# Order of the weight sums, the first evacuation and the activation sums in a Winograd feed-forward layer

## The chip, the cores and the metric

One Trainium2 chip, one NeuronCore. The time is device microseconds of one execution; the median of the runs is the figure that is compared.

## What is computed

One layer of a hybrid encoder on 2,048 prompt rows and 32 sample rows, all in float32. Attention and a gated linear attention come first; the change lies in the feed-forward part that follows, a gated MLP with a causal convolution of width 3 between its two matrix products (D_MODEL is 1024, D_FF 2816):

```python
def conv_ffn(h, conv_state, w_up, w_dw, b_dw, w_down):
    t = h.shape[1]
    u = h @ w_up
    uu = jnp.concatenate([conv_state.astype(u.dtype), u], axis=1)
    y = b_dw
    for j in range(CONV_W):
        y = y + w_dw[j] * uu[:, j:j + t]
    a, g = jnp.split(y, 2, axis=-1)
    out = (jax.nn.gelu(a, approximate=True) * g) @ w_down
    return out, uu[:, -(CONV_W - 1):]
```

## The kernel before

**Units and blocks.** The feed-forward part runs from about 1838 us of the profiled span to its end. It is twelve units. Units 0 to 2 are the up product for the row groups p = 0, 1, 2, with 22 column pairs each; the other nine are the down product, for three row groups times three pieces g of the inner dimension, with 4 column pairs each (units 3 to 5 belong to p = 0). `block` handles one column pair. Below, up0, up1 and up2 are the three up units, and down0 the three down units of p = 0.

**One block.** Each column pair is a 2x2 block product in the Winograd form of Strassen's scheme: seven products instead of eight, of the weight operands A11, S2, S1, S3, A12, S4, A22 with the row operands B11, T2, T1, T3, B21, B22, T4. `prod` (the matmul line is L1561) is one of them: 12 matmuls on TensorE (PE), since every float32 operand is split in a high and a low part. The block's text order is: A11·B11 into ad0; ScalarE (ACT) copies ad0 to g0 (L1656); then `prev()`, the rest of the block before (its product A22·T4, its convolution of g, its gate product); then S2·T2 into g0 and the copy U2 (L1662); S1·T1 and the copy P5 (L1665); S3·T3 and the add to g1 (L1668, VectorE, DVE); A12·B21; S4·B22 and the add to ad1 (L1679, DVE). Then ad is evacuated: in an up unit by `conv` (L1575 on ACT, twice L1577 on DVE) and Gelu (L1687), in a down unit by `down_sum`.

**Side work.** Between the products stands `side()`, seven times in a block. It issues deferred transfers, steps the rows' preparation (`hstep`: loads of `ht` and their splits) and takes one step of the generator `weights()` (`next(wq)`). Such a step makes one weight operand ready: `part` calls `split`, which writes the high part on ACT (L67) and the low part on DVE (L70) into a ring of places (`hA`, `hB`, `ring`).

**Weight sums.** S1 = A21 + A22, S2 = S1 − A11, S3 = A11 − A21 and S4 = A12 − S2 are made once, in the blocks of row group 0 (22 columns of up0 and 12 of down0, 34 in all): S1, S2 and S3 by GpSimd (POOL, L1512), S4 by DVE (also L1512). They are stored to DRAM (`sW`, `sD`; L1515) and loaded again for the other row groups. The raw weights stand in eight buffers (`raws`, loads at L1490); `free` and `freed` list those to be filled.

**Activation sums.** After every second block of an up unit, `act_sums` makes the row operands' sums for the down product out of two stored activations (`work` tiles; L1599 to L1602 on DVE); the activations go to `actD`, their sums to `aT` (L1590). The sums overwrite the tile of which `actD` is written, so they wait for those stores.

**What sets the order.** A building framework schedules each engine's instructions: the text's order is the priority, and it moves an instruction up or down where its model says that another is ready first. Each engine then runs its list in that order, waiting at each entry for semaphores. Where an instruction ends up is seen in the built program alone.

Of the kernel before, what the change touches and what calls it, by code (L numbers as in the profile page):

```python
# [13 lines left out]
AF = mybir.ActivationFunctionType  # L14
# [25 lines left out]
def dap(ap, offset, dims):  # L40
    return bass.AP(tensor=ap.tensor, offset=ap.offset + offset, ap=dims)
# [17 lines left out]
def encoder_step(ctx: ExitStack, tc: tile.TileContext, I, O):  # L59
# [520 lines left out]
    with ExitStack() as st:  # L580
# [188 lines left out]
        def step(gen):  # L769
            if gen is not None:  # L770
                next(gen, None)
# [690 lines left out]
    def raw(i, n=4):  # L1462
        return raws_[:, 512 * i:512 * i + 128 * n].rearrange("p (k n) -> p k n", n=128)
# [12 lines left out]
    def weights():  # L1476


        todo = []
        for u, (p, g) in enumerate(UNITS):  # L1480
            for m in range(NM[u]):
                todo += [(u, m, x) for x in (("A21", "A22", "A11", "A12") if p == 0 else WOPS)]
        at = {}

        def fetch():

            while todo and free and len(at) < NRAW - 2:
                u, m, x = todo.pop(0)
                at[u, m, x] = i = free.pop(0)
                nc.sync.dma_start(raw(i, NK[u]), w_rows(u, m, x))  # L1490

        freed = []

        def refill():

            free.extend(freed)
            freed.clear()
            fetch()

        def part(u, m, x, i):  # L1500
# [9 lines left out]
        def total(u, m, eng, op, out, a, b):  # L1510
            n = NK[u]
            getattr(eng, op)(raw(out, n), raw(a, n), raw(b, n))  # L1512

        def keep(u, m, x, i):
            nc.sync.dma_start(w_rows(u, m, x), raw(i, NK[u]))  # L1515

        fetch()
        for u, (p, g) in enumerate(UNITS):
            for m in range(NM[u]):
                if p == 0:  # L1520
                    a11, a12, a21, a22 = [at.pop((u, m, x)) for x in ("A11", "A12", "A21", "A22")]
                    free.extend(freed)
                    freed.clear()
                    s1, s2 = free.pop(0), free.pop(0)
                    total(u, m, nc.gpsimd, "tensor_add", s1, a21, a22)
                    total(u, m, nc.gpsimd, "tensor_sub", s2, s1, a11)
                    total(u, m, nc.gpsimd, "tensor_sub", a21, a11, a21)
                    fetch()
                    for x, i in zip(WOPS, (a11, s2, s1, a21, a12, a12, a22)):
                        if x == "S4":  # L1530
                            total(u, m, nc.vector, "tensor_sub", a12, a12, s2)
                            freed.append(s2)
                        yield from part(u, m, x, i)
                        if x == "S1":
                            keep(u, m, "S2", s2)
                        if x in SUM and x != "S2":
                            keep(u, m, x, i)
                        yield
                        refill()
                        if x not in ("S2", "A12"):  # L1540
                            freed.append(i)
                else:
                    for x in WOPS:
                        i = at.pop((u, m, x))
                        yield from part(u, m, x, i)
                        yield
                        refill()
                        freed.append(i)

    wq = weights()  # L1550

# [40 lines left out]

    def act_sums():

        while made:
            p, j, x, y = made.pop(0)
            o = WP[p] - 2
            x0, x1, y0, y1 = x[:, 0, :o], x[:, 1, :o], y[:, 0, :o], y[:, 1, :o]
            nc.vector.tensor_sub(x0, x1, x0)  # L1599
            nc.vector.tensor_sub(x1, y1, x1)  # L1600
            nc.vector.tensor_sub(y1, y1, x0)
            nc.vector.tensor_sub(y0, y0, y1)  # L1602
            for i, v in ((0, x), (2, y)):
                defer(0 if p == 2 and j == MF // 2 - 1 else 1,
                      dap(aT, ((4 * p + i) * 11 + j) * 128 * SEG, [[SEG, 128], [11 * 128 * SEG, 2], [1, o]]), v[:, :, :o])

    def up_g(p, m, g, ya, before):

        o = WP[p] - 2
        conv(YG, g, m + MF, o)  # L1610
        nc.vector.tensor_mul(ya[:, :, :o], ya[:, :, :o], YG[:, :, :o])
        defer(1, actD[p, m, :, :, :o], ya[:, :, :o])
        if m % 2:
            made.append((p, m // 2, before, ya))

    xs = {}
    ORDER = (0, 4, 1, 5, 2, 6, 3, 7)
# [26 lines left out]
    def block(u, m, prev, side):  # L1644
# [27 lines left out]
        if u == 2:  # L1672
            conv_outputs(g[:, 1], m + MF)
# [6 lines left out]
        if u == 2:  # L1680
            conv_outputs(ad[:, 1], m)
        if grp is None:
            YA.append(YA.pop(0))
            before, ya = YA[-2:]
            o = w - 2
            conv(ya, ad, m, o)
            nc.scalar.activation(ya[:, :, :o], ya[:, :, :o], AF.Gelu_apprx_tanh)  # L1687
        else:
# [131 lines left out]
    def side():  # L1820
        issue()
        step()
        next(wq, None)
        hstep()
        pend()

    f2 = prev = None
    for u, (p, grp) in enumerate(UNITS):
        for m in range(NM[u]):
# [15 lines left out]
            if u == 0 and f2 is None and not queue:  # L1845
                s3.close()
                f2 = pool(ctx, "ff2")
                fr = f2.tile([128, 2 * 1024], F32R, name="ring")
                sa, sq = [f2.tile([128, 2, SEG], F32, name=x) for x in ("saF", "sqF")]
                acc2 = f2.tile([128, 12 * SEG], F32, name="acc2")  # L1850
                spare = [x[:, 2 * SEG * c:2 * SEG * c + 2 * SEG].rearrange("p (s w) -> p s w", w=SEG)
                         for x, n in ((work, 5), (acc2, 6)) for c in range(n)]
# [72 lines left out]
```

## Time and profile before

| | before |
|---|---|
| median of 3 runs | 3352.89 us (3344.52 to 3361.07) |
| profiled execution, own time | 3328.72 us |
| its span | 3327.0 us |
| mean granted clock of TensorE | 0.981 |
| busy: PE, DVE, ACT, POOL | 94%, 68%, 50%, 17% |

The span is the time that the trace covers, the own time that of the same execution as the runs are timed; it is 24 us below the runs' median. The granted clock is a share of TensorE's full speed.

### The profile page before, as it was taken

To read this page: it belongs to the slowest core of one execution; us is meant where nothing else is said; L and a number is where in the kernel's file an instruction comes from. 1 tells how busy PE (TensorE), PEld (TensorE's weight loads), DVE (VectorE), ACT (ScalarE), POOL (GpSimd) and SP (SyncE) were. 2 spreads that over 40 slices of the span, in tenths; PEclk is the share of its full clock that TensorE was granted. 3 is DMA by queue.
4 is the path that set the end of the run, shared out by engine and by line. 5 is a ranking of instruction groups with operands and counts; after the bars stand their busy time and mean duration, and the time that the engine had idled before them with its cause. 6 is when DMAs were issued, how large, how long until landed. Compare 5 with 4: busy or idle time off the path is not lost. (4 is left out here: it accounts for less than half of the span.)

```text
span 3327.0 us, 58007 instructions
## 1 busy us (share of the span) xinstructions
PE 3134.7 (94%) x19928; PEld 2979.6 (90%) x19928; DVE 2264.7 (68%) x4858; ACT 1673.4 (50%) x3835; POOL 573.0 (17%) x687
## 2 busy tenths in 40 slices
PE   6999999999999999899999798999999999899996
PEld 5899998888999999889988787999999999899996
DVE  6725527664545555754777887887778778788886
ACT  4412224443455545533545644465556656566755
POOL 3102101111111111112444323210000001221011
PEclk8999999999999999999999999999999999999998
DMA  7334434445333333654565786576668666769794
GB/s 216 113 121 142 128 110 120 126 129 138 107 109 113 111 106 114 206 169 155 166 213 172 234 263 223 189 238 193 185 183 242 192 191 194 232 208 294 222 284 125
DMA packets 601370, 580.25 MB, mean 174 GB/s; under 512 B 55761, under 2 KB 529570, under 8 KB 601074
## 3 DMA queue, kind: packets, MB, share of 16 engines
q1 hardware_dynamic: 556386, 528.93, 53.1%
q10 hardware_dynamic: 44432, 47.34, 4.4%
q8 instruction: 157, 2.57, 0.3%
q14 instruction: 139, 1.14, 0.1%
q0 software_dynamic: 256, 0.26, 0.0%
HBM read 388.71 MB, written 187.65 MB: 173 GB/s over the span
## 5 line engine op out<-in xcount | busy, mean ns | idle before, releaser
L76 PE MATMUL pm<-hA,wh 128*128 128x416 f32 x768 | 288.2, 375 | 0.0
L67 ACT ACTIVATE hA<-raws 128x512 fp32r<-128x512 f32 (+1 forms) x320 | 196.5, 617 | 180.7 <-PE ad L1561 96.8
L77 PE MATMUL pm<-hA,wh 128*128 128x416 f32 x768 | 269.4, 351 | 0.0
L78 PE MATMUL pm<-hA,wl 128*128 128x416 f32 x768 | 269.2, 351 | 0.0
L1561 PE MATMUL ad<-hA,hB 128*128 128x350 f32 (+2 forms) x1533 | 264.4, 323 | 0.9 <-ACT work L1665 0.7
L1561 PEld LDWEIGHTS ad<-hA,hB 128*128 128x128 f32 x1533 | 249.4, 189 | 1.8 <-ACT work L1665 1.7
L1512 POOL TENSOR_TENSOR raws<-raws 128x512 f32<-128x512 f32 (+1 forms) x102 | 147.6, 1460 | 587.2 <-DVE g L1571 284.6
L70 DVE TENSOR_TENSOR hA<-raws,hA 128x512 fp32r<-128x512 f32 (+1 forms) x320 | 229.6, 720 | 28.0 <-ACT hA L67 26.8
L67 ACT ACTIVATE hB<-raws 128x512 fp32r<-128x512 f32 (+1 forms) x240 | 147.0, 616 | 131.2 <-PE ad L1561 68.0
L934 POOL TENSOR_SCALAR P<-P,mx 128x640 f32<-128x640 f32 (+5 forms) x136 | 101.3, 745 | 544.0 <-DVE mx L933 269.1
L1561 PE MATMUL g<-hA,hB 128*128 128x350 f32 (+2 forms) x954 | 171.8, 330 | 20.4 <-ACT g L1656 9.7
L1561 PE MATMUL ad<-hA 128*128 128x350 f32 (+2 forms) x1047 | 182.9, 325 | 2.0 <-ACT work L1665 2.0
L70 DVE TENSOR_TENSOR hB<-raws,hB 128x512 fp32r<-128x512 f32 (+1 forms) x240 | 168.6, 705 | 22.9 <-ACT hB L67 20.8
L1561 PEld LDWEIGHTS g<-hA,hB 128*128 128x128 f32 x954 | 157.6, 192 | 26.5 <-ACT g L1656 13.4
L76 PE MATMUL pn<-wh,hA 128*128 128x256 f32 (+1 forms) x624 | 177.8, 285 | 0.0
L1561 PE MATMUL ad<-hA,hA 128*128 128x348 f32 (+2 forms) x1014 | 177.8, 325 | 0.0
L78 PE MATMUL pn<-wh,hA 128*128 128x256 f32 (+1 forms) x624 | 176.7, 283 | 0.0
L77 PE MATMUL pn<-wl,hA 128*128 128x256 f32 (+1 forms) x624 | 176.7, 283 | 0.0
L1561 PEld LDWEIGHTS ad<-hA 128*128 128x128 f32 x1047 | 171.8, 191 | 2.3 <-ACT work L1665 2.3
L1561 PE MATMUL ad<-hA,ring 128*128 128x348 f32 (+2 forms) x978 | 169.5, 324 | 1.3 <-ACT work L1665 1.3
L67 ACT ACTIVATE pth<-pp 128x256 fp32r<-128x256 f32 (+1 forms) x288 | 106.1, 373 | 126.3 <-PE pp L1001 116.3
L1561 PEld LDWEIGHTS ad<-hA,hA 128*128 128x128 f32 x1014 | 166.6, 191 | 0.1
(437 smaller groups left out, 9168.9 us busy)
## 6 DMA issues: line engine op xcount, KB each, us to landing
raws<-in_w_up_dram SPq DMA_DIRECT2D x220, 256.0 KB, 3.7
raws<-sW SPq DMA_DIRECT2D x176, 256.0 KB, 3.0
sW<-raws SPq DMA_DIRECT2D x88, 256.0 KB, 3.2
raws<-in_w_down_dram SPq DMA_DIRECT2D x80, 256.0 KB, 4.6
wr<-in_w_in_dram SPq DMA_DIRECT2D x76, 256.0 KB, 3.4
sgT<-tx ACTq DMA_DIRECT2D x80, 208.0 KB, 2.3
wa<-in_w_ada_dram SPq DMA_DIRECT2D x64, 256.0 KB, 3.1
keys<-ks SPq DMA_DIRECT2D x128, 128.0 KB, 2.9
```

Source lines behind the costliest of these rows:

```text
L67: i = nc.scalar.activation(hi, src, AF.Copy)
L70: nc.vector.tensor_sub(lo, src, f32(hi))
L76: nc.tensor.matmul(out, ah, bh, start=first and i == 0, stop=False)
L77: nc.tensor.matmul(out, ah, bl, start=False, stop=False)
L78: nc.tensor.matmul(out, al, bh, start=False, stop=last and i == n - 1)
L934: nc.gpsimd.tensor_scalar(P[:m, :tot], P[:m, :tot], mx[:m, 6:7], 1.0, op0=OP.mult, op1=OP.mult)
L1512: getattr(eng, op)(raw(out, n), raw(a, n), raw(b, n))
L1561: nc.tensor.matmul(out[:, :w], l_[:, k], r_[:, k, :w], start=first and k == 0 and i == 0, stop=k == n - 1 and i == 2, skip_group_check=True)
```

## The change

It edits five things. (1) `weights()` is written anew: GpSimd's three sums of a column are emitted at operand S4 of the column before (`total3(cur + 1)`), only column 0's still right before its own use; S4 is computed at operand S3 and written over S2's buffer instead of A12's; each sum's store stands right behind its split; loads are emitted for no more than one column ahead, without the earlier limit of six buffers. (2) The evacuation of ad (`conv`, Gelu, `conv_outputs`, or `down_sum`) moves into `rest()`, so that in the text it stands after the next block's first product and copy. (3) `act_sums` runs one column pair later, and its stores are always deferred by one step. (4) `side()` calls `hstep()` ahead of `next(wq)`. (5) The list of spare row buffers of one stage begins with the other tensor.

```diff
-        todo = []
-        for u, (p, g) in enumerate(UNITS):
-            for m in range(NM[u]):
-                todo += [(u, m, x) for x in (("A21", "A22", "A11", "A12") if p == 0 else WOPS)]
-        at = {}
+        cols = [(u, m) for u in range(len(UNITS)) for m in range(NM[u])]
+        fresh = [UNITS[u][0] == 0 for u, m in cols]
+        todo = [(c, x) for c in range(len(cols)) for x in (("A21", "A22", "A11", "A12") if fresh[c] else WOPS)]
+        at, freed = {}, []
+        cur = -1
         def fetch():
-            while todo and free and len(at) < NRAW - 2:
-                u, m, x = todo.pop(0)
-                at[u, m, x] = i = free.pop(0)
-                nc.sync.dma_start(raw(i, NK[u]), w_rows(u, m, x))
+            while todo and free and todo[0][0] <= cur + 1:
+                c, x = todo.pop(0)
+                at[c, x] = i = free.pop(0)
+                nc.sync.dma_start(raw(i, NK[cols[c][0]]), w_rows(*cols[c], x))
...
+        def total3(c):
+            free.extend(freed)
+            freed.clear()
+            at[c, "S1"], at[c, "S2"] = s1, s2 = free.pop(0), free.pop(0)
+            at[c, "S3"] = a21 = at.pop((c, "A21"))
+            total(c, nc.gpsimd, "tensor_add", s1, a21, at[c, "A22"])
+            total(c, nc.gpsimd, "tensor_sub", s2, s1, at[c, "A11"])
+            total(c, nc.gpsimd, "tensor_sub", a21, at[c, "A11"], a21)
...
-                    s1, s2 = free.pop(0), free.pop(0)
-                    total(u, m, nc.gpsimd, "tensor_add", s1, a21, a22)
-                    total(u, m, nc.gpsimd, "tensor_sub", s2, s1, a11)
-                    total(u, m, nc.gpsimd, "tensor_sub", a21, a11, a21)
-                    fetch()
-                    for x, i in zip(WOPS, (a11, s2, s1, a21, a12, a12, a22)):
-                        if x == "S4":
-                            total(u, m, nc.vector, "tensor_sub", a12, a12, s2)
-                            freed.append(s2)
-                        yield from part(u, m, x, i)
-                        if x == "S1":
-                            keep(u, m, "S2", s2)
-                        if x in SUM and x != "S2":
-                            keep(u, m, x, i)
-                        yield
-                        refill()
...
+        for cur in range(len(cols)):
+            u, m = cols[cur]
+            for x in WOPS:
+                if x == "A11" and fresh[cur] and (cur, "S1") not in at:
+                    total3(cur)
+                if x == "S3" and fresh[cur]:
+                    at[cur, "S4"] = at[cur, "S2"]
+                    total(cur, nc.vector, "tensor_sub", at[cur, "S4"], at[cur, "A12"], at[cur, "S4"])
+                if x == "S4" and cur + 1 < len(cols) and fresh[cur + 1]:
+                    total3(cur + 1)
+                i = at[cur, x]
+                yield from part(cur, x, i)
+                if fresh[cur] and x in SUM:
+                    nc.sync.dma_start(w_rows(u, m, x), raw(i, NK[u]))
+                yield
+                refill()
...
     def act_sums():
-        while made:
+        if made and made[0] is None:
+            made.pop(0)
+        elif made:
             p, j, x, y = made.pop(0)
...
         if m % 2:
-            made.append((p, m // 2, before, ya))
+            made.extend((None, (p, m // 2, before, ya)))
...
         nc.vector.tensor_add(ad[:, 1, :w], ad[:, 1, :w], U2[:, :w])
-        if grp is None:
-            YA.append(YA.pop(0))
-            before, ya = YA[-2:]
-            o = w - 2
-            conv(ya, ad, m, o)
-            nc.scalar.activation(ya[:, :, :o], ya[:, :, :o], AF.Gelu_apprx_tanh)
-        else:
+        if last:
             down_sum(p, grp, m, ad, m == 0)
         side()
 
         def rest():
+            if grp is None:
+                YA.append(YA.pop(0))
+                before, ya = YA[-2:]
+                o = w - 2
+                if u == 2:
+                    conv_outputs(ad[:, 1], m)
+                conv(ya, ad, m, o)
+                nc.scalar.activation(ya[:, :, :o], ya[:, :, :o], AF.Gelu_apprx_tanh)
+            elif not last:
+                down_sum(p, grp, m, ad, m == 0)
             prod(g[:, 0], u, m, "A22", "T4", False)
...
     def side():
         issue()
         step()
+        hstep()
         next(wq, None)
-        hstep()
         pend()
```

The built programs show where this puts the instructions. First ACT, in up0, from the evacuation of one block's ad to the copy U2 of the next (that is block 15 of 22), before:

```order
L1575 ACTIVATE work_22385<-ad_24428,cw_21930 128x2x348 [waits DMAHW7_49,DVE_49]
L67 ACTIVATE hB1_677<-raws_21938 128x512 [waits PE_49,Pool_49]
L1656 COPY g_24571<-ad_24570 128x350 [waits PE_49,Activation_49]
L67 ACTIVATE hB1_677<-raws_21938 128x512 [waits PE_49,Pool_49]
L1687 ACTIVATE work_22385<-work_22385 128x2x348 [waits DVE_49]
L1575 ACTIVATE work_22385<-g_24429,cw_21930 128x2x348 [waits PE_49]
L67 ACTIVATE hA0_104<-raws_21938 128x512 [waits PE_49,Pool_49]
L1662 COPY work_22385<-g_24571 128x350 [waits PE_49,Activation_49]
```

The same place of the changed program (its lines for L1575, L1687 are L1571, L1690):

```order
L1571 ACTIVATE work_22386<-ad_24425,cw_21930 128x2x348 [waits DMAHW0_49,DVE_49]
L67 ACTIVATE hB1_677<-raws_21938 128x512 [waits PE_49,Pool_49]
L1656 COPY g_24562<-ad_24561 128x350 [waits PE_49,Activation_49]
L67 ACTIVATE hB1_677<-raws_21938 128x512 [waits PE_49,Pool_49]
L1690 ACTIVATE work_22386<-work_22386 128x2x348 [waits DVE_49]
L1571 ACTIVATE work_22386<-g_24426,cw_21930 128x2x348 [waits PE_49]
L67 ACTIVATE hA0_104<-raws_21938 128x512 [waits PE_49]
L1662 COPY work_22386<-g_24562 128x350 [waits PE_49,Activation_49]
```

The order is the same: the convolution of ad stands ahead of the copy L1656 in both, although the text has it behind (so it is in 62 of the 66 up blocks, before in 63). The last split no longer waits for GpSimd, and the two that do wait there wait for sums that GpSimd was given one block earlier: the sums of column 14, for one, followed DVE's low part behind the g add of block 12 before, and now that behind the ad add of block 11.

Next DVE in the same block, from the g add (L1668) on, before:

```order
L1668 TENSOR_TENSOR g_24571<-g_24571,work_22385 128x350 [waits PE_49,Activation_49]
L1512 TENSOR_TENSOR raws_21938<-raws_21938 128x512 [waits DVE_49]
L70 TENSOR_TENSOR hA0_104<-raws_21938,hA0_104 128x512 [waits Activation_49]
L70 TENSOR_TENSOR ring_22896<-raws_21938,ring_22896 128x512 [waits DMAHW0_49,PE_49,Activation_49]
L1599 TENSOR_TENSOR work_22385<-work_22385 128x348 [waits DMAHW2_49]
L1679 TENSOR_TENSOR ad_24570<-ad_24570,work_22385 128x350 [waits PE_49]
```

and with the change (L1679 is now L1677, L1577 is L1573, L1512 is L1499, L1599 is L1598):

```order
L1668 TENSOR_TENSOR g_24562<-g_24562,work_22386 128x350 [waits PE_49,Activation_49]
L70 TENSOR_TENSOR hA0_104<-raws_21938,hA0_104 128x512 [waits Activation_49]
L70 TENSOR_TENSOR ring_22887<-raws_21938,ring_22887 128x512 [waits DMAHW3_49,PE_49,Activation_49]
L1598 TENSOR_TENSOR work_22386<-work_22386 128x348 [waits DMAHW5_49,DVE_49]
L1677 TENSOR_TENSOR ad_24561<-ad_24561,work_22386 128x350 [waits PE_49]
L70 TENSOR_TENSOR ring_22887<-raws_21938,ring_22887 128x512 [waits DMAHW6_49,Activation_49]
L1573 SCALAR_TENSOR_TENSOR work_22386<-ad_24561,cw_21930,work_22386 128x2x348 [waits Activation_49]
L70 TENSOR_TENSOR hA1_105<-raws_21938,hA1_105 128x512 [waits PE_49,Activation_49]
L1573 SCALAR_TENSOR_TENSOR work_22386<-ad_24561,cw_21930,work_22386 128x2x348 [waits DVE_49]
L70 TENSOR_TENSOR hA1_105<-raws_21938,hA1_105 128x512 [waits PE_49,Activation_49]
L1499 TENSOR_TENSOR raws_21938<-raws_21938 128x512 [waits DMAHW4_49,DMAHW0_49,DVE_49]
```

S4 has gone from between the two adds to behind the next block's convolutions of ad, and there it waits for two transfers (A12's load and the store of S2, whose buffer it overwrites).

Last DVE in up1, block 31, where nothing is summed and `act_sums` has its turn, before:

```order
L1668 TENSOR_TENSOR g_26636<-g_26636,work_22385 128x348 [waits PE_49,Activation_49]
L70 TENSOR_TENSOR hA1_105<-raws_21938,hA1_105 128x512 [waits DMAHW2_49,Activation_49]
L1599 TENSOR_TENSOR work_22385<-work_22385 128x346 [waits DMAHW4_49,DVE_49]
L70 TENSOR_TENSOR hB1_677<-raws_21938,hB1_677 128x512 [waits DMAHW5_49,PE_49,Activation_49]
L1679 TENSOR_TENSOR ad_26635<-ad_26635,work_22385 128x348 [waits PE_49]
```

and with the change:

```order
L1668 TENSOR_TENSOR g_26627<-g_26627,work_22386 128x348 [waits PE_49,Activation_49]
L70 TENSOR_TENSOR hA1_105<-raws_21938,hA1_105 128x512 [waits DMAHW2_49,Activation_49]
L1598 TENSOR_TENSOR work_22386<-work_22386 128x346 [waits DMAHW4_49,DVE_49]
L70 TENSOR_TENSOR hB1_677<-raws_21938,hB1_677 128x512 [waits PE_49,Activation_49]
L1677 TENSOR_TENSOR ad_26626<-ad_26626,work_22386 128x348 [waits PE_49]
```

The first of the activation sums stands at the same place with the same wait for a store. On SP, which issues the transfers, the stores of S2, S1 and S3 now stand behind one another and ahead of the next loads, where before loads stood between them.

## Rows read from the trace of the kernel before

**Rows 1.** The page's first part: busy time, share of the span and instructions of PE.
```profile
PE 3134.7 (94%) x19928; PEld 2979.6 (90%) x19928; DVE 2264.7 (68%) x4858; ACT 1673.4 (50%) x3835; POOL 573.0 (17%) x687
```

**Rows 2.** Busy time by stretch of the span: the stretch and its length, then busy us and instructions of each engine, PE's granted clock, the DMA engines' busy share and GB/s. The first three are up0 (22 blocks), the fourth is up1, the fifth a part of up2, the last down0.
```profile
1840.00:1886.00 46.00, 33.19 (x174) 31.64 (x173) 43.69 (x70) 32.10 (x57) 19.88 (x19) 0.85 0.68 211
1886.00:2075.00 189.00, 161.83 (x924) 156.68 (x924) 158.01 (x229) 94.56 (x164) 54.57 (x47) 0.95 0.78 245
2075.00:2209.00 134.00, 125.95 (x756) 121.34 (x756) 109.29 (x156) 72.66 (x124) 33.55 (x23) 1.00 0.63 199
2209.00:2514.00 305.00, 297.61 (x1842) 294.29 (x1843) 241.96 (x367) 178.26 (x300) 0.27 (x4) 1.00 0.69 199
2570.00:2787.00 217.00, 217.00 (x1350) 216.70 (x1349) 171.39 (x289) 131.32 (x274) 0.00 (x0) 1.00 0.64 190
2819.00:2990.00 171.00, 155.24 (x918) 152.30 (x919) 134.75 (x185) 100.99 (x183) 45.93 (x33) 0.96 0.69 215
```

**Rows 3.** What PE waited for in 1886 to 2209 us (up0 from its third block): us in total, times, longest.
```profile
PE g L1561 <- ACT g L1656: 18.9, 13, 3.0
PE g L1561 <- ACT work L1662: 10.0, 9, 2.6
PE ad L1561 <- ACT work L1665: 2.2, 2, 2.0
```

**Rows 4.** The timeline around the start of block 11: start, duration, engine, line, operation, operands, count, and in brackets the idle time before it and what ended it.
```profile
2037.63 0.93 ACT L1575 ACTIVATE work<-ad,cw 128x696 f32<-128x696 f32 x1 [1.39 <-DVE ad L1679]
...
2038.46 0.45 ACT L1656 COPY g<-ad 128x350 f32<-128x350 f32 x1
...
2038.97 2.19 PE L1561 MATMUL g<-hA,hB 128*128 128x350 f32 x12 [1.41 <-ACT g L1656]
2039.46 4.35 POOL L1512 TENSOR_TENSOR raws<-raws 128x512 f32<-128x512 f32 x3 [11.84 <-DMA sW<-raws]
2040.78 0.63 ACT L67 ACTIVATE hB<-raws 128x512 fp32r<-128x512 f32 x1 [1.86 <-POOL raws L1512]
...
2042.15 0.63 ACT L67 ACTIVATE hA<-raws 128x512 fp32r<-128x512 f32 x1 [0.74 <-POOL raws L1512]
...
2043.84 0.63 ACT L67 ACTIVATE hB<-raws 128x512 fp32r<-128x512 f32 x1 [0.24 <-POOL raws L1512]
...
2045.05 0.43 ACT L1662 COPY work<-g 128x350 f32<-128x350 f32 x1
...
2045.53 3.42 PE L1561 MATMUL g<-hA,hB 128*128 128x350 f32 x12 [2.43 <-ACT work L1662]
```

**Rows 5.** The splits' line L67 in 1886 to 2209 us: how long ACT sat idle before them (us, times), by what ended it.
```profile
  POOL raws L1512: 36.7, 33
...
  DVE raws L1512: 20.0, 8
...
  DMA raws<-in_w_up_dram: 7.3, 5
```

**Rows 6.** The same for the convolution's line L1575 in 1886 to 2209 us.
```profile
  DVE ad L1679: 20.5, 14
```

**Rows 7.** What PE waited for in 2819 to 2990 us (down0).
```profile
PE g L1561 <- ACT work L1662: 11.0, 5, 3.2
PE g L1561 <- ACT g L1656: 5.5, 4, 3.4
PE ad L1561 <- ACT work L1665: 1.8, 2, 1.3
```

**Rows 8.** ACT's idle time before the splits L67 in 2819 to 2990 us, by what ended it.
```profile
  POOL raws L1512: 14.1, 11
  DMA ht<-actD: 11.3, 7
  DMA ht<-aT: 7.0, 4
  DVE raws L1512: 6.9, 5
```

**Rows 9.** What PE waited for most in 2209 to 2514 us (up1).
```profile
PE g L1561 <- ACT g L1656: 7.3, 8, 1.4
```

**Rows 10.** What DVE waited for there, of the activation sums.
```profile
DVE work L1599 <- DMA actD<-work: 22.0, 10, 2.8
...
DVE work L1601 <- DMA actD<-work: 15.8, 10, 2.5
```

**Rows 11.** The timeline of the next block's start: GpSimd's three sums and DVE beside them.
```profile
2055.59 4.87 POOL L1512 TENSOR_TENSOR raws<-raws 128x512 f32<-128x512 f32 x3 [11.78 <-DVE work L1599]
2055.92 1.51 DVE L70 TENSOR_TENSOR ring<-raws,ring 128x512 fp32r<-128x512 f32 x1
...
2059.22 0.93 DVE L1577 SCALAR_TENSOR_TENSOR work<-ad,cw,work 128x696 f32<-128x696 f32 x1
```

**Rows 12.** DVE's groups in 2570 to 2787 us, where GpSimd does nothing: busy us, mean ns of one, idle before.
```profile
L70 DVE TENSOR_TENSOR hA<-raws,hA 128x512 fp32r<-128x512 f32 x50 | 34.2, 685 | 0.0
L1577 DVE SCALAR_TENSOR_TENSOR work<-ad,cw,work 128x696 f32<-128x696 f32 x33 | 31.0, 940 | 17.0 <-ACT work L1575 17.0
```

**Rows 13.** DVE's S4 in 1886 to 2075 us, in the same columns.
```profile
L1512 DVE TENSOR_TENSOR raws<-raws 128x512 f32<-128x512 f32 x11 | 10.7, 974 | 2.7 <-POOL raws L1512 2.7
```

**Rows 14.** The sums' stores in 1840 to 2209 us: line, operation, count, KB of one, median us from issue to landing.
```profile
sW<-raws SPq DMA_DIRECT2D x84, 256.0 KB, 3.2
```

More of the change, by code (lines that the diff above doesn't have):

```diff
@@ L1498, in refill, with total, part @@
             fetch()
-        def part(u, m, x, i):
+        def total(c, eng, op, out, a, b):
+            n = NK[cols[c][0]]
+            getattr(eng, op)(raw(out, n), raw(a, n), raw(b, n))
+        def total3(c):
[6 more added lines that the diff above has]
+            total(c, nc.gpsimd, "tensor_sub", a21, at[c, "A11"], a21)
+        def part(c, x, i):
+            u, m = cols[c]
             while True:
@@ L1508, in part @@
             split(hi[:, :n], lo[:, :n], raw(i, n))
[L1510 to L1515, printed above, removed]
-        fetch()
[L1518 to L1523, printed above, removed]
-                    s1, s2 = free.pop(0), free.pop(0)
-                    total(u, m, nc.gpsimd, "tensor_add", s1, a21, a22)
-                    total(u, m, nc.gpsimd, "tensor_sub", s2, s1, a11)
-                    total(u, m, nc.gpsimd, "tensor_sub", a21, a11, a21)
-                    fetch()
-                    for x, i in zip(WOPS, (a11, s2, s1, a21, a12, a12, a22)):
-                        if x == "S4":
-                            total(u, m, nc.vector, "tensor_sub", a12, a12, s2)
-                            freed.append(s2)
-                        yield from part(u, m, x, i)
-                        if x == "S1":
-                            keep(u, m, "S2", s2)
-                        if x in SUM and x != "S2":
-                            keep(u, m, x, i)
-                        yield
-                        refill()
-                        if x not in ("S2", "A12"):
-                            freed.append(i)
-                else:
[L1543 to L1548, printed above, removed]
@@ new lines, in weights @@
+        fetch()
+        for cur in range(len(cols)):
[14 more added lines that the diff above has]
+                refill()
+                if not (fresh[cur] and x == "S2"):
+                    freed.append(i)
+                del at[cur, x]
+                if x == "S2" and fresh[cur]:
+                    at[cur, "S2"] = i
+            at.pop((cur, "S2"), None)
@@ L1603, in act_sums @@
             for i, v in ((0, x), (2, y)):
-                defer(0 if p == 2 and j == MF // 2 - 1 else 1,
-                      dap(aT, ((4 * p + i) * 11 + j) * 128 * SEG, [[SEG, 128], [11 * 128 * SEG, 2], [1, o]]), v[:, :, :o])
+                defer(1, dap(aT, ((4 * p + i) * 11 + j) * 128 * SEG, [[SEG, 128], [11 * 128 * SEG, 2], [1, o]]), v[:, :, :o])
     def up_g(p, m, g, ya, before):
         o = WP[p] - 2
+        if p == 2:
+            conv_outputs(g[:, 1], m + MF)
         conv(YG, g, m + MF, o)
@@ L1671, in block @@
             down_sum(p, grp, m + 4, g, False, 1)
-        if u == 2:
-            conv_outputs(g[:, 1], m + MF)
         side()
@@ L1679, in block @@
         nc.vector.tensor_add(ad[:, 1, :w], ad[:, 1, :w], U2[:, :w])
-        if u == 2:
-            conv_outputs(ad[:, 1], m)
-        if grp is None:
-            YA.append(YA.pop(0))
-            before, ya = YA[-2:]
-            o = w - 2
-            conv(ya, ad, m, o)
-            nc.scalar.activation(ya[:, :, :o], ya[:, :, :o], AF.Gelu_apprx_tanh)
-        else:
+        if last:
             down_sum(p, grp, m, ad, m == 0)
@@ L1851, in encoder_step @@
                 spare = [x[:, 2 * SEG * c:2 * SEG * c + 2 * SEG].rearrange("p (s w) -> p s w", w=SEG)
-                         for x, n in ((work, 5), (acc2, 6)) for c in range(n)]
+                         for x, n in ((acc2, 6), (work, 5)) for c in range(n)]
                 RING[:] = [(fr, 1024 * i) for i in range(2)] + [(fA[0], 11200 + 1024 * i) for i in range(2)] \
```

1 line of the change is left out of this document (removed).

## The prediction

> **What bounds the kernel now.** I began with the page's busy shares: PE is busy 94% of the span [rows 1], so a change can only give back what is missing there, or what the clock costs. Next I cut the feed-forward part into stretches [rows 2]. The fifth row, a part of up2 without weight sums, is the yardstick: 1350 matmuls in 217.00 us, busy throughout, at clock 1.00, so 0.1607 us for each. Up1 is nearly as good: 297.61 of 305.00 us busy. The stretches in which sums are made are not: PE is busy 161.83 of 189 us, 125.95 of 134 us, and in down0 155.24 of 171 us. In two of them the granted clock is below full as well (0.95 and 0.96: part of the time PE ran at 1.2 GHz instead of 2.4); the stretches where it hardly waits are at 1.00.
>
> Third, the waits. In up0 from its third block on PE waits for three ACT copies: 18.9 us for the first copy L1656, 10.0 for U2, 2.2 for P5, 31.1 together [rows 3]. The copies are late because ACT, which runs its list in order, stands before something ahead of them. The timeline shows both kinds [rows 4]: the convolution of ad waits 1.39 us for DVE's add, the copy L1656 follows at 2038.46, and PE has lost 1.41 us. Then GpSimd begins three sums at 2039.46; three splits on ACT wait 1.86, 0.74 and 0.24 us for them; U2 comes only at 2045.05, and PE loses 2.43 us. Over the stretch ACT's splits idle 36.7 us for GpSimd's sums and 20.0 for DVE's [rows 5], the convolution 20.5 us for the add [rows 6]. Down0 has the same picture: PE waits 11.0, 5.5 and 1.8 us [rows 7], the splits 14.1 + 6.9 us for sums, but also 11.3 + 7.0 us for the rows' loads [rows 8].
>
> **The change, part by part.**
>
> Weight sums. No sum is removed or added: three on GpSimd and one on DVE for each of 34 columns. They get their inputs about a block sooner, in blocks of some 15 us (756 matmuls are 9 blocks of 84, in 134 us [rows 2]), while the longest single stall that they make is of the order of 2 us [rows 4]; so the stall on sums should go nearly whole, and the question is how much PE gets of it. Of ACT's idle time that stands before the copies, the sums' share in up0 is (36.7 + 20.0) / (36.7 + 20.0 + 20.5) = 0.73 [rows 5, 6]. I give U2 and P5 that share: 12.2 x 0.73 = 8.9 us. Before L1656 the convolution of ad stands last, waiting for the add; S4 (0.97 us with contention [rows 13]) leaves DVE's list ahead of that add, and the sums' stalls no longer delay the row, but the wait itself remains. I give it half the share, 0.365: 18.9 x 0.365 = 6.9 us. Together 15.8 of 31.1 us, 51%. The clock cost about (1 − 0.95) x 189 = 9.5 us; I give back the same share, 4.8. Up0: **20.6 us**. The bounds are nothing and 31.1 + 9.5 = 40.6.
>
> The first 46 us of up0 I leave at zero: DVE is busy 43.69 of them [rows 2], and column 0's sums still stand right before their use, so an earlier sum finds no free DVE. If that is wrong, it is 12.8 us of idle PE at most.
>
> Down0: sums 21.0 of 39.3 us, 0.53 [rows 8]. U2 and P5 12.8 x 0.53 = 6.8, L1656 5.5 x 0.27 = 1.5, so 8.3 of 18.3 us, 45%; clock (1 − 0.96) x 171 = 6.8, of which 3.1. **11.4 us**, bounds nothing and 25.1.
>
> Evacuation of ad behind the copy: zero. The built program still has the convolution ahead of the copy at the place shown, as in nearly all blocks. Had it moved, it could give up to the wait before L1656, 18.9 us in up0 and 7.3 in up1 [rows 3, 9]; that is in the second rival. Activation sums a pair later: zero. In up1 they stand where they stood, and the waits of 22.0 + 15.8 us for the stores on DVE [rows 10] stay; they cost PE little anyway, since DVE is busy 241.96 of 305 us and PE idles 7.4 [rows 2]. Rows ahead of weights and the spare order: zero; PE has no idle time left in the yardstick stretch to be won there [rows 2]. They are covered by splits a block ahead of use; with the cover gone, a late row load costs PE what ACT now idles for such loads in down0, 18.3 us [rows 8].
>
> S4 into S2's buffer: a new wait on DVE, for the store of S2. A store takes 3.2 us to land [rows 14]. Below it is nothing, if S2's store lands during the rest of the splits (in the built list S4 has moved ten DVE instructions down); above it is 3.2 us in each of 34 columns, 109 us, on everything queued behind S4: the convolution of g, its gate product and the low parts of the next operands. I take nothing, since S2 is now made a block earlier and stored first, and keep the end for the range. The loads of the next column, now issued behind three stores on SP, have the same cover: ACT waits for raw loads only 7.3 us today [rows 5].
>
> Contention. While GpSimd's three sums ran, a low part took 1.51 us; without them it takes 0.685 [rows 11, 12]. The convolution's step, with one input in PSUM, took 0.93 beside 0.94. So the sums keep their price on DVE, wherever they stand. In 1886 to 2075 DVE is busy 158.01 of 189 us [rows 2]: whatever the order, this stretch can give back no more than 31 us, and DVE would have to run without a gap for that.
> The Trainium skill, GPSIMD Engine Reference, section 1 (Specifications), says that GpSimd shares its SBUF interfaces with VectorE and contends with DVE instructions that have two SBUF inputs. The trace agrees, 1.51 against 0.685 us, and by that rule the sum count, which does not change, sets DVE's load; the sum would then be the first rival's.
>
> **Sum.** 20.6 + 11.4 = 32.0 us off the profiled execution's own 3328.72, 3296.7. Its time lies 24.2 us under the runs' median 3352.89; I take the difference to the median: **3321 us**.
>
> **Rivals.**
> DVE stays the bound. In up0's second stretch nothing is won because DVE, stretched by the sums, is the last to finish. For it: 84% busy there, 95% in the first [rows 2]; against it: up1 runs PE at 98% with DVE at 79%, and 31 us of DVE are free. Left are the third stretch, (134 − 125.95) x 0.51 = 4.1 us, and down0's 11.4: 15.5 us, 3337.
>
> Everything comes back. If DVE's add arrives sooner as well, since S4 and the stalls are gone from its path, both copies are on time: 40.6 + 25.1 = 65.7 us, 3287. For it: add and copies wait on one another in a ring, so a stall removed is removed again in the next block; against it: the convolution still stands before the copy.
>
> The wait only moves. The change limits loads to one column ahead, and puts three stores ahead of them; if raw weights come late by what the sums did, the splits wait for transfers instead. For it: the DMA engines are 78% busy in 1886 to 2075 [rows 2]. It gives 3353.
>
> Slower: the wait on S2's store. DVE stands at S4 with the convolutions and the splits behind it. The point from which it decides is 32.0 / 34 = 0.94 us per column on the path of PE; at the full 3.2 us it would be 3353 − 32 + 109 = 3430, at half of that 3375. For it: store and load waits are what stalls DVE in up1 [rows 10]; against it: the store is issued a block sooner.
>
> **How the numbers follow.** The forecast has 0.45, DVE as the bound 0.18, everything back 0.12, the moved wait 0.15, the slower case 0.10. 0.5%, 17 us, is about what a measurement of this kernel can tell from no change, so the limits are 3336 and 3370. Faster: 0.43 of the forecast, 0.09 of DVE's bound (it falls on the limit), 0.12: 0.64. Same: 0.02 + 0.09 + 0.12: 0.23. Slower: 0.10 + 0.03: 0.13. The range 3283 to 3350 leaves out the slower case, half of the moved wait and 0.03 of the case that brings everything, 0.20 in all.
>
> **Signs in the profile after.** ACT's idle time for GpSimd's sums in up0 falls from 36.7 to under 5 us; PE's wait for U2 there from 10.0 to under 4, while that for L1656 stays at 10 or more. Up1 keeps its 305 us, its 7.3 us before L1656 and DVE's 38 us for `actD`. DVE's low parts beside GpSimd's sums still take 1.5 us. DVE waits for stores to `sW` under 5 us in all; if this reads 30 or more, the slower case holds. Clock 0.97 or more in 1886 to 2075. The prediction is wrong if the first copy's wait goes or grows with the list order unchanged, if splits wait for `raws` loads over 20 us, or if up1 or up2 changes its length by over 5 us.

## The result, and the profile after

The changed kernel takes 3358.69 us in the median (20 runs), the kernel before 3348.97 beside it (20 runs): ratio 1.0029, interval 1.0020 to 1.0039. It is slower by some 10 us, and it lies outside the forecast's range of 3283 to 3350.

By units the two profiled executions read as follows: in the order up0, up1, up2, down0 and the rest (down1 and down2), the stretch and its length, busy us of PE, PEld, DVE, ACT and POOL, clock, DMA share, GB/s. Before:

```profile
1840.20:2209.30 369.10, 320.82 (x1853) 309.67 (x1853) 311.09 (x453) 199.42 (x343) 107.80 (x87) 0.95 0.71 224
2209.30:2514.20 304.90, 297.81 (x1843) 294.49 (x1844) 241.86 (x367) 178.16 (x300) 0.27 (x4) 1.00 0.69 198
2514.20:2819.40 305.20, 299.53 (x1855) 297.75 (x1853) 248.06 (x412) 188.75 (x390) 4.81 (x4) 1.00 0.68 204
2819.40:2990.00 170.60, 155.24 (x918) 152.30 (x919) 134.75 (x185) 100.59 (x183) 45.53 (x33) 0.96 0.69 215
2990.00:3300.53 310.53, 300.36 (x1852) 295.66 (x1850) 253.31 (x360) 206.81 (x374) 31.45 (x30) 0.99 0.79 241
```

After:

```profile
1848.20:2221.60 373.40, 321.37 (x1853) 311.28 (x1853) 321.93 (x454) 196.58 (x339) 112.61 (x84) 0.95 0.70 221
2221.60:2530.60 309.00, 299.01 (x1844) 294.59 (x1845) 240.25 (x365) 177.82 (x300) 0.27 (x4) 1.00 0.68 196
2530.60:2850.10 319.50, 306.58 (x1849) 297.78 (x1848) 249.34 (x408) 184.60 (x388) 9.77 (x6) 0.99 0.67 195
2850.10:3014.10 164.00, 152.82 (x924) 149.98 (x923) 137.59 (x190) 101.21 (x185) 43.59 (x30) 0.98 0.73 225
3014.10:3332.91 318.81, 303.10 (x1853) 296.80 (x1851) 251.85 (x360) 206.36 (x374) 29.79 (x30) 0.99 0.76 235
```

Up0 is 4 us longer, up1 4, up2 14, down0 7 shorter, the rest 8 longer. (The up product's first matmul also comes 7.5 us later in the second execution, at 1845.3 instead of 1837.8 us. Of these, 3.0 lie ahead of the first weight load, which the change does not touch, and 4.5 between that load and the matmul, where the new `weights()` already runs: this stretch takes 24 to 25 us in the five profiles of this document that have the old one and 27 to 29 in the nine that have the new. No row of a unit holds it. The profiled execution of before lies 20 us under the median of its runs, that of the changed kernel near its median; so for the size of an effect the ratios of the runs count, and the units' lengths say where it lies.)

What PE waited for in up0 from its third block on, after:

```profile
PE g L1557 <- ACT g L1656: 31.5, 18, 3.1
PE ad L1557 <- ACT work L1665: 3.7, 3, 1.6
PE g L1557 <- ACT work L1662: 3.6, 3, 1.7
```

and DVE, first before, then after:

```profile
DVE work L1599 <- DMA actD<-work: 7.3, 5, 2.6
DVE work L1601 <- DMA actD<-work: 5.2, 3, 2.4
```
```profile
DVE work L1598 <- DMA actD<-work: 13.7, 4, 3.8
DVE work L1600 <- DMA actD<-work: 12.6, 6, 3.0
```

The wait for U2 has gone from 10.0 to 3.6 us, and that for the first copy from 18.9 to 31.5 [rows 3]: the sum of the three copies is 31.1 before and 38.8 after. DVE's waits for the stores of activations have doubled, from 12.5 to 26.3 us. ACT's idle time before the splits in that stretch:

```profile
  POOL raws L1499: 12.6, 10
  DVE raws L1499: 10.4, 4
```

and before the convolution of ad:

```profile
  DVE ad L1677: 51.4, 18
```

ACT idles 23.0 us for weight sums instead of 56.7 [rows 5], and 51.4 us for DVE's ad add instead of 20.5 [rows 6]. The stall was not removed, it went to the ad add. The timeline of block 16 shows why, after:

```profile
2129.13 4.89 POOL L1499 TENSOR_TENSOR raws<-raws 128x512 f32<-128x512 f32 x3 [12.52 <-DVE hB L70]
...
2130.91 1.97 DVE L1611 TENSOR_TENSOR work<-work 128x696 f32<-128x696 f32 x1
...
2138.60 0.52 DVE L1600 TENSOR_TENSOR work<-work 128x348 f32<-128x348 f32 x1 [2.99 <-DMA actD<-work]
2139.04 0.53 DVE L1677 TENSOR_TENSOR ad<-ad,work 128x350 f32<-128x350 f32 x1
...
2139.60 0.93 ACT L1571 ACTIVATE work<-ad,cw 128x696 f32<-128x696 f32 x1 [3.55 <-DVE ad L1677]
...
2140.95 0.45 ACT L1656 COPY g<-ad 128x350 f32<-128x350 f32 x1
...
2141.45 2.19 PE L1557 MATMUL g<-hA 128*128 128x350 f32 x12 [2.10 <-ACT g L1656]
```

and SP's queue in that time:

```profile
2126.89 7.48 SPq L1536 DMA_DIRECT2D sW<-raws  x4
2134.46 0.94 SPq L1586 DMA_DIRECT2D actD<-work  x1
```

Read it backwards. PE waits 2.10 us for the copy; the copy stands behind the convolution of ad; that waits 3.55 us for the ad add; the add stands on DVE behind an activation sum (L1600); and the sum waits 2.99 us for the store of the activation, `actD`. This store is late twice over. The gate product L1611 that makes the activation runs beside GpSimd's three sums and takes 1.97 us; it ends at 2132.88. And SP issues the store at 2134.46 only, behind four stores of weight sums, of which the last waits for GpSimd's third sum (to 2134.02). Before, in block 15, where it is the first of the four activation sums (L1599) that waits ahead of the ad add:

```profile
2112.17 0.88 DVE L1611 TENSOR_TENSOR work<-work 128x696 f32<-128x696 f32 x1
...
2113.07 0.53 SPq L1590 DMA_DIRECT2D actD<-work  x1
...
2116.90 0.52 DVE L1599 TENSOR_TENSOR work<-work 128x348 f32<-128x348 f32 x1 [0.78 <-DMA actD<-work]
```

The product took 0.88 us, SP issued 0.02 us after its end, and the sum waited 0.78. With the change the same sum of block 15 waits 3.40 us:

```profile
2121.17 0.52 DVE L1598 TENSOR_TENSOR work<-work 128x348 f32<-128x348 f32 x1 [3.40 <-DMA actD<-work]
```

### The profile page after: what moved, and what is told of

It is laid out like the page before. It is cut to its first block, busy times and chain, and to the rows that moved or that the text cites. A ratio compares the mean times of both kernels' runs of the same rounds, so it can differ in the third digit from the quotient of the medians.

```text
span 3360.5 us, 58153 instructions
## 1 busy us (share of the span) xinstructions
PE 3148.1 (94%) x19928; PEld 2983.2 (89%) x19928; DVE 2277.0 (68%) x4858; ACT 1670.5 (50%) x3835; POOL 586.2 (17%) x687
## 5 line engine op out<-in xcount | busy, mean ns | idle before, releaser
L67 ACT ACTIVATE hA<-raws 128x512 fp32r<-128x512 f32 (+1 forms) x320 | 196.3, 617 | 163.3 <-PE ad L1557 101.1
L70 DVE TENSOR_TENSOR hA<-raws,hA 128x512 fp32r<-128x512 f32 (+1 forms) x320 | 239.0, 749 | 30.9 <-ACT hA L67 27.5
L1499 POOL TENSOR_TENSOR raws<-raws 128x512 f32<-128x512 f32 (+1 forms) x102 | 156.2, 1542 | 592.3 <-DVE hB L70 347.5
L67 ACT ACTIVATE hB<-raws 128x512 fp32r<-128x512 f32 (+1 forms) x240 | 146.8, 616 | 119.4 <-PE ad L1557 73.2
L70 DVE TENSOR_TENSOR hB<-raws,hB 128x512 fp32r<-128x512 f32 (+1 forms) x240 | 176.0, 737 | 14.6 <-ACT hB L67 12.4
L67 ACT ACTIVATE pth<-pp 128x256 fp32r<-128x256 f32 (+1 forms) x288 | 106.3, 374 | 126.1 <-PE pp L1001 119.3
```

The source lines that it names most:

```text
L67: i = nc.scalar.activation(hi, src, AF.Copy)
L70: nc.vector.tensor_sub(lo, src, f32(hi))
```

## The experiments

The ratio is to the kernel before, run beside each on the same chip; 3 to 10 runs of each kernel stand behind it (20 for the change). The kernel before has medians of 3335 to 3349 us in the four sets of runs. Lengths are those of the units in one profiled execution, in us: up1, in which outputs_back and the change have the same instructions, reads 305 and 309, so a difference of 4 us between two rows says little by itself.

| kernel | ratio (interval) | up0 | up1 | up2 | down0 | down1+2 |
|---|---|---|---|---|---|---|
| before | 1 | 369 | 305 | 305 | 171 | 311 |
| the change | 1.0029 (1.0020–1.0039) | 373 | 309 | 320 | 164 | 319 |
| sums_only | 0.9994 (0.9982–1.0005) | 368 | 308 | 306 | 160 | 313 |
| sums_undone | 1.0036 (1.0022–1.0050) | 370 | 306 | 313 | 172 | 315 |
| stores_on_act | 1.0029 (1.0017–1.0042) | 366 | 305 | 315 | 166 | 321 |
| act_sums_pinned | 0.9898 (0.9880–0.9915) | 349 | 296 | 298 | 166 | 319 |
| before_pinned | 0.9952 (0.9935–0.9968) | 370 | 299 | 303 | 171 | 311 |
| later_pinned_alone | 0.9931 (0.9913–0.9949) | 362 | 297 | 300 | 176 | 313 |
| undone_pinned | 0.9951 (0.9934–0.9969) | 365 | 296 | 300 | 179 | 313 |
| conv_pinned | 0.9894 (0.9879–0.9908) | 346 | 298 | 298 | 170 | 317 |
| short_sums | 0.9821 (0.9803–0.9838) | 332 | 296 | 298 | 153 | 317 |
| outputs_back | 0.9968 (0.9955–0.9981) | 373 | 305 | 302 | 160 | 318 |
| rows_after | 0.9891 (0.9876–0.9905) | 346 | 298 | 298 | 163 | 318 |
| pinned_stores_act | 0.9915 (0.9898–0.9932) | 353 | 296 | 301 | 167 | 322 |

**The change in two halves.** sums_only is before with the new `weights()` (the first two pieces of the diff above and the loop); sums_undone is the change with the old one.

> The kernel before with the new weights() alone (edit 1); evacuation, activation sums and side() as before. Theory A (two separate effects: edit 1 moves up0's wait from U2 to the first copy, edits 2 to 5 lengthen up2 by its conv_outputs): up0 as with the whole change, about 373 us with 9 us before U2 and over 25 us before L1656; up2 back at 305 to 308 us; time about 3346, ratio 0.999 to the kernel before. Rival B (up2 is longer because the new loads of weights come later): up2 stays at 319 us and the time at 3358.

> The changed kernel with the old weights(): edits 2 to 5 alone. Theory A: up0 as before, 369 us with 20 us before U2 and 20 us before L1656; up2 about 319 us; time about 3360, ratio 1.004. Rival B: up2 at 305 us, time about 3349. A third outcome, up0 under 360 us, would say that edits 2 to 5 help up0 and that edit 1 takes it away.

Theory A held in the main. 0.9994 and 1.0036 add up to the whole change: edit 1 is worth nothing here, and edits 2 to 5 cost 12 us. In sums_only up0 keeps its length while PE's waits move (U2 19.9 to 7.0 us over the unit, L1656 19.5 to 30.8); only down0 gains, 11 us. DVE's waits for `actD` in up0 from its third block on, 12.5 us before, are 23.2 in sums_only and 12.5 in sums_undone: it is edit 1 that doubles them. In sums_undone up2 is 8 us longer than before, at 313 us; theory A had 319 and B 305, so there A is right in kind and not in size.

**The sums' stores off SP.**

```diff
-                    nc.sync.dma_start(w_rows(u, m, x), raw(i, NK[u]))
+                    nc.scalar.dma_start(w_rows(u, m, x), raw(i, NK[u]))
```

> The changed kernel; the stores of the weight sums are issued by ScalarE's queue behind the split of each sum instead of SP's. Theory C (in up0 the store of the activation waits on SP behind the sums' stores, so the activation sum, the ad add behind it on DVE, the convolution and the first copy come late): DVE's waits for actD in up0 fall from 26 us to under 15, PE's wait for L1656 there from 33 to under 20, the time to about 3345, ratio 0.999. Rival D (GpSimd's sums, now beside the gate product, stretch DVE's work and that alone makes the add late): both waits stay within 20% and the time within 5 us of 3359.

DVE's waits in up0 from its third block on:

```profile
DVE work L1600 <- DMA actD<-work: 5.2, 5, 2.6
...
DVE work L1598 <- DMA actD<-work: 2.7, 5, 1.2
```

26.3 us became 7.9: SP's order is most of what delays `actD` in up0, as theory C says. The rest of its forecast missed: PE's wait for L1656 rose over the unit from 32.6 to 38.6 us, and the time stayed at 1.0029. The stores now stand in ACT's own list ahead of its next split and copy. By the starts of the copies L1656, a block from 10 to 15 takes 15.0 us against 16.7 with the change, but the first four take 85 us against 79. So what delays the store is shown. That the remedy costs as much on ACT as it gives is likely, but not shown: with the sums pinned the same move costs 0.0017, some 6 us (pinned_stores_act, below).

**The activation sums really a pair later.**

```diff
-            nc.vector.tensor_sub(x0, x1, x0)
+            tc.keep_in_program_order(nc.vector.tensor_sub(x0, x1, x0))
```

and so for all four; the scheduler may then not move them up past DVE work of earlier text.

> The changed kernel with the four activation sums of a pair kept in text order on DVE, so that they really stand one column pair later. Theory C (the waiting activation sum ahead of the ad add is what delays the copy): DVE's waits for actD fall to under 3 us in each of up0, up1 and up2 (from 26, about 38 and 31), PE's wait for L1656 from 33 to under 15 us in up0, from 10 to under 4 in up1; time about 3335, ratio 0.996. Rival D: the waits for actD go as well, but the copy stays late, since the ad add is late for DVE's own work; PE's wait for L1656 in up0 stays over 25 us and the time within 5 us of 3359.

The units in the order of above:

```profile
1843.60:2192.90 349.30, 312.64 (x1853) 303.87 (x1853) 325.26 (x452) 195.59 (x338) 115.38 (x84) 0.98 0.76 234
2192.90:2489.30 296.40, 294.93 (x1840) 294.36 (x1841) 247.17 (x365) 179.38 (x302) 0.27 (x4) 1.00 0.69 205
2489.30:2786.90 297.60, 297.48 (x1851) 297.19 (x1850) 247.05 (x404) 187.60 (x386) 8.49 (x6) 1.00 0.69 207
2786.90:2952.40 165.50, 152.50 (x927) 149.04 (x926) 143.33 (x196) 101.70 (x188) 44.25 (x31) 0.99 0.75 231
```

DVE has no wait for `actD` left in any unit. Up0 is 24 us shorter than with the change, up1 13, up2 22, at clock 0.98 to 1.00; PE's wait for L1656 is 17 us in up0 (theory C had under 15) and 0.5 in up1. The first of the sums now starts 10 to 22 us behind the gate product that ends its pair, where with the change it started in the mean 7 us ahead of it. The ratio is lower than theory C had (0.996). Four orderings of instructions that cost nothing turn 1.0029 into 0.9898, and this kernel beats both.

Is it the pinning or the pair? before_pinned pins the sums where the old text has them; later_pinned_alone adds edit 3 alone and pins. (In the second, without edit 5, the last pair's tiles can be taken for the down units' rows before its sums are made, so values of the last sums differ; number and sizes of the instructions do not.)

> The kernel before with its four activation sums kept in text order, one block behind their pair and not later. Theory C (what helps is that the sums stand far enough behind the activation's store): right behind the pair the store of its second half has only just been issued, so DVE's waits for actD stay at 30 us or more in up1, and the time stays within 0.4% of before. Rival E (being kept from floating upwards is enough by itself): the waits go and the ratio is about 0.990.

> The kernel before with edit 3 alone (activation sums one column pair later), the sums kept in text order; weight sums, evacuation and side() as before. Theory C: DVE's waits for actD go in all three up units, up1 and up2 fall to about 297 us, up0 to about 355; ratio 0.989 to 0.992. Rival F (the gain of the pinned kernel needs the new weights() or the other edits too): ratio 0.996 or more.

before_pinned: waits for `actD` of 10.3 us in up1, where theory C had 30 or more, and half of the gain, 0.9952. So being kept from floating upwards gives part by itself. later_pinned_alone: all waits gone, up1 at 297, but up0 at 362, ratio 0.9931, between the two forecasts. The 11 us from there to 0.9898 are the other edits together; the next run takes edit 1 out of them.

**What edit 1 is worth with that wait gone.** undone_pinned is act_sums_pinned with the old `weights()`.

> The changed kernel with the old weights() and the activation sums kept in text order. Against the pinned kernel with the new weights() (0.9898) it gives the worth of edit 1 with the waits for actD out of the way. Theory L (edit 1 does give back part of the stalls for the sums, and the wait for actD hid it): up0 360 us or more against 349, PE's wait for U2 there 17 us or more, ratio 0.993 to 0.995. Rival M (edit 1 is worth nothing, DVE bounds up0): up0 within 4 us of 349, ratio 0.990.

Up0 and down0:

```profile
1842.10:2207.50 365.40, 321.65 (x1853) 312.31 (x1853) 314.55 (x454) 199.17 (x343) 107.33 (x87) 0.95 0.71 224
...
2803.30:2982.10 178.80, 156.12 (x918) 152.95 (x919) 136.88 (x190) 101.46 (x187) 47.59 (x33) 0.95 0.68 211
```

Theory L holds, with the ratio at the upper edge of its forecast and PE's wait for U2 at 17.6 us: edit 1 is worth 16.1 us in up0 (365.4 to 349.3) and 13.3 in down0, of which 6 are given back in down1 and down2 and some 4 by the later start of the up product; in the runs 0.0053, 18 us with an interval of some 8 to either side. Without the pinning the same edit is worth 0.0007, 2 us (sums_undone 1.0036, the change 1.0029). The change as it was made had the gain and lost it again behind `actD`.

**The other places.** conv_pinned queues the convolution of ad behind the next block's copy, rows_after puts `hstep()` back, pinned_stores_act issues the sums' stores on ACT; all three have the sums pinned.

```diff
conv_pinned, in rest():
-                conv(ya, ad, m, o)
+                with tc.issue_after(first_copy[0]):
+                    conv(ya, ad, m, o)
rows_after, in side():
-        hstep()
         next(wq, None)
+        hstep()
```

> The changed kernel with the activation sums kept in text order and the convolution of ad really behind the next block's copy L1656 on ScalarE (edit 2 made effective). Theory G (in up0 the convolution's wait for the ad add is what is left of the first copy's delay): PE's wait for L1656 in up0 falls from 17 to under 4 us, up0 from 349 to about 338; ratio to the kernel before 0.986. Rival H (ACT's convolution, Gelu and DVE's gate product come later by as much and hold the next copies): up0 and up1 no shorter, ratio 0.990 or more.

> The changed kernel with the activation sums kept in text order and with hstep() behind next(wq) in side() again (edit 4 undone). If rows first cost the 2 to 6 us that the first units of down1 and down2 are longer, these come back to 60 us each and the ratio is about 0.988; if not, 0.990 and no unit changes by over 3 us.

> The changed kernel with the activation sums kept in text order and the weight sums' stores on ScalarE's queue. Theory C (SP's order mattered only through the wait for actD, which is gone here): no gain, up0 within 4 us of 349 or longer by what the issues cost ACT, ratio 0.990 to 0.993. Rival (the stores on SP also hold back loads that PE waits for): up0 under 343 us, ratio 0.988 or less.

With the convolution behind the copy PE's wait for L1656 in up0 falls from 17.2 to 4.2 us, but that for U2 rises from 11.5 to 22.1: the delay is handed to the next copy, and 0.9894 is no different from 0.9898. Rival H is right on the mechanism, though up0 did get 3.6 us shorter. rows_after is the same within its interval (0.9891), and down1 and down2 stay as long; what lengthens them by 6 us when the new weights and the other edits meet is open. Stores on ACT gain nothing here (0.9915, up0 353).

**GpSimd's sums beside DVE.** short_sums lets each GpSimd sum cover a quarter of its columns from the fifth column pair on.

```diff
             n = NK[cols[c][0]]
+            if eng is nc.gpsimd and c >= 4:
+                n = 1
```

> The changed kernel with the activation sums kept in text order; from the fifth column on GpSimd's three sums cover 128 of 512 columns only, so three quarters of that work is left out. It prices GpSimd's sums beside DVE in up0 and down0. Theory D (DVE stretched by the sums bounds up0): the gate product L1611 takes 0.9 instead of 2.0 us, up0 falls from 349 to 335 us or less, ratio 0.986 or less. Rival: the stretched DVE work is off PE's path once the activation sums stand later; up0 within 4 us of 349.

The gate product in up0 from its third block on (busy us, mean ns, idle), in act_sums_pinned (with the change the row reads the same) and in short_sums:

```profile
L1611 DVE TENSOR_TENSOR work<-work 128x696 f32<-128x696 f32 x20 | 27.4, 1369 | 0.1
```
```profile
L1613 DVE TENSOR_TENSOR work<-work 128x696 f32<-128x696 f32 x20 | 17.8, 888 | 0.1
```

Up0 falls by 17.6 us and down0 by 13, theory D's size. Shorter sums are also ready sooner, but that is the smaller part in up0: ACT's idle time before the splits for GpSimd's sums falls from 9.2 to 3.2 us there, that before the convolution for DVE's ad add from 32.4 to 10.0. With the waits for `actD` gone, the sums' length is thus most of what down0 has above PE's own time (some 149 us for 927 matmuls at 0.1607), and a third of that in up0 (some 297 us at the same rate). Work is left out here, so this is a price and no gain that could be had.

**Up2.** outputs_back puts the two calls of `conv_outputs` back where they were, ahead of the evacuation and out of `rest()`.

```diff
+        if u == 2:
+            conv_outputs(g[:, 1], m + MF)
         side()
         prod(ad[:, 0], u, m, "A12", "B21", False)
...
         nc.vector.tensor_add(ad[:, 1, :w], ad[:, 1, :w], U2[:, :w])
+        if u == 2:
+            conv_outputs(ad[:, 1], m)
```

> The changed kernel with conv_outputs at its two old places in up2 (behind the g add and behind the ad add), all else as changed. Theory K (in up2 the copies for conv_outputs stand ahead of Gelu and of g's convolution, so the gate product, its store, the activation sum behind that store and the ad add come about 2 us later): the gate product starts 5.5 us after the first copy as before, not 7 to 8, up2 falls from 319 to about 306 us, ratio 0.999. Rival: up2 stays over 314 us, since the longer unit comes from the loads or the rows' order.

Theory K holds, and the ratio is lower than it had: up2 is at 302, ratio 0.9968, 20 us better than the change. Before, a block in up2 reads (copy, gate product):

```profile
2651.72 0.45 ACT L1656 COPY g<-ad 128x350 f32<-128x350 f32 x1
...
2657.26 0.88 DVE L1611 TENSOR_TENSOR work<-work 128x696 f32<-128x696 f32 x1
```

and after:

```profile
2687.21 0.45 ACT L1656 COPY g<-ad 128x350 f32<-128x350 f32 x1
...
2695.13 0.88 DVE L1611 TENSOR_TENSOR work<-work 128x696 f32<-128x696 f32 x1
...
2700.28 0.52 DVE L1598 TENSOR_TENSOR work<-work 128x348 f32<-128x348 f32 x1 [2.37 <-DMA actD<-work]
```

and in outputs_back:

```profile
2643.95 0.45 ACT L1654 COPY g<-ad 128x350 f32<-128x350 f32 x1
...
2649.48 0.88 DVE L1609 TENSOR_TENSOR work<-work 128x696 f32<-128x696 f32 x1
```

The gate product starts 7.9 us behind the copy instead of 5.5; over the blocks of up2 the median is 7.2 after, 5.5 before and in outputs_back. The two small ACT copies out of g and DVE's write into it now stand ahead of Gelu and g's convolution. The store is late by that much, and the same chain follows: activation sum, ad add, convolution, copy. DVE's waits for `actD` in up2 are in sum no longer than before (30.9 against 32.0 us); what grows is ACT's wait for the ad add, from 12.3 to 30.0 us. In act_sums_pinned the gate product is as late, 7.2 us, and up2 takes 298 us: the lateness costs PE by way of the activation sums alone.

## Why the prediction was wrong

*Stalls for weight sums.* Right in mechanism. ACT's idle time for them fell by 33.7 us, though to 12.6 for GpSimd's and not under 5; PE's wait for U2 fell to 3.6, forecast under 4. Of the 32.0 us forecast for edit 1 the runs show 18 (the units 29.4 in up0 and down0, less what is given back elsewhere), and only once the wait for `actD` is away. Even there the split is another: of the 16.1 us in up0, PE's idle time gives 7.1 and its busy time at the higher clock 9.0, where the forecast had 15.8 and 4.8. That up0's total comes near its 20.6 is in part luck.

*The first copy, 18.9 x 0.365 = 6.9 us given back.* This is the step that failed: the wait rose by 12.6, to 31.5 us. The share was taken of ACT's idle time as if its causes ran one after another. They ran side by side: behind the stall for sums, DVE's ad add was waiting in its own queue for a store, and edit 1 made that wait twice as long. I had listed those waits and written that they "cost PE little anyway", since DVE is idle a fifth of up1. But DVE's free time says nothing of the instructions queued behind the wait. The ad add stood there, and act_sums_pinned shows the price: up1 alone is 8.5 us shorter than before without them.

*Stores on SP at nothing, under cover of loads that are early.* I asked what of the loads came late behind three stores, not what of the activation's store did. That is the rival "the wait only moves", with another transfer than I named, and by edit 1 alone it comes out at that rival's no change (sums_only, 0.9994).

*GpSimd's sums keep their price on DVE.* Right in kind: the gate product takes 1.97 us beside the sums, 0.88 without. The Trainium skill, GPSIMD Engine Reference, section 1 (Specifications), says that GpSimd contends with DVE instructions that have two SBUF inputs; the trace agrees, since the gate product has two. What I missed is that a sum moved in time meets another instruction: before, the splits; now the gate product, on which the store hangs. The first rival, DVE as the bound, was wrong in form, since the pinned kernel keeps all of DVE's work, 325 us in up0, and has up0 at 349 us.

*Up2.* The forecast's second failure: this unit had no term at all, and is 14 us longer. Without that the change is 11 us faster than before (outputs_back, 0.9968), so this is what gave the result its sign. I followed the order of instructions in up0 and up1 and left out the unit in which the moved `conv_outputs` runs; its copies now stand ahead of g's convolution there and put it back, and with it the gate product.

*The rest.* The evacuation did stay ahead of the copy, and moving it really is worth nothing (conv_pinned). DVE's wait for S2's store is 0.9 us in up0, so the slower rival's mechanism did not occur. Down0 gave 6.6 us of the 11.4 forecast, and 10.8 with edit 1 alone. The clock in up0 stayed at 0.95, where I had given back half of its loss. The first weights cost some 4 us more before the up product begins; that had no term either.

## What to carry to other kernels

Before a stall is booked as won, ask which queue the next-latest input of the same consumer stands in, and what each wait on that queue holds up behind it: an engine with a fifth of its time free can still delay everything behind one wait for a store. A transfer issued on a shared queue inherits the waits of those ahead of it, so when stores are moved, look for the store that is urgent and now stands last (here one that was ready at 2132.88 us and issued at 2134.46). Price moved code in every stage in which it runs: here the one unit without a term decided the sign. And where a scheduler decides, text moved later may not move at all; find out in the built order, and pin what matters.

## What was unexpected of the hardware

The time that two engines take from one another changed hands with the order: in up0 from its third block on, GpSimd's sums took 1492 ns each before and 1604 after (spans on GpSimd are rough in these profiles), while DVE's gate product went from 929 to 1369 ns in the mean and S4 from 851 to 725.
